# Products of the second group of 32 inverted blocks, moved from stages 3 and 4 of the last head pair to stages 5 and 6

## The chip, the cores and the metric

One NeuronCore of one Trainium2 chip runs the whole kernel. The metric is device time in microseconds (us) for one execution. Engines are named as in the profile: PE (TensorE matmuls), PEld (its weight loads), DVE (VectorE), ACT (ScalarE), POOL (GpSimd), SP (SyncE, which issues most DMAs). Each engine works through its own list of instructions in order, and waits when the next one's input, or the buffer it writes, isn't ready.

## What is computed

One layer of a diffusion transformer on 512 latent tokens and 256 context tokens, model width 1024: normalisation and modulation, one input projection, two groups of heads side by side (neighbourhood attention and a bidirectional RWKV-7 scan), an output projection, and a mixture of 32 experts. The part that matters here is the scan of the second group:

```
def step(S, inp):
    r_t, w_t, kk_t, akk_t, k_t, v_t = inp
    S = (S * w_t[:, :, None, :]
         - jnp.einsum('bhvk,bhk->bhv', S, kk_t)[..., None] * akk_t[:, :, None, :]
         + v_t[..., None] * k_t[:, :, None, :])
    return S, jnp.einsum('bhvk,bhk->bhv', S, r_t)
```

The kernel works it in chunks of 64 tokens. For each chunk, direction and head a 64 x 64 unit triangular matrix has to be inverted; the inverses (tile `TT`, array `TTd` in HBM) are used later, when the scan runs chunk by chunk.

## The kernel before

The program has three long parts: preparation (to about 430 us: normalisation, projections, everything that the scan needs), scan and attention (to about 710 us), and the experts. The change lies in the preparation.

**Pairs, units, stages.** The 8 scan heads are handled as 4 pairs, `p` = 0 to 3 (`rw_pair`). A pair has 4 units: 2 directions by 2 halves of the 12 chunks. The loop over `n` = 2 to 6 in `rw_pair` is what this text calls stages 2 to 6. In stage `n`, `coupling` multiplies out the blocks of unit `n - 3` (PE, tile `pmg`; DVE copies the diagonal blocks masked into `ND`, ACT the others into `NO`), `decayed` makes the operands `AR` and `BK` of unit `n - 2` (ACT, DVE, POOL), and `decay` starts unit `n - 1` (PE tiles `psg` and `paf`, ACT, and a scan on DVE into `sig`).

**The inversion.** Units deliver 96 blocks in all, which are inverted in three groups of 32 (b = 0, 1, 2); group 1 is complete late in pair 2, group 2 in stage 6 of pair 3. `solve_a` inverts the 32 x 32 diagonal blocks of a group by elimination on DVE alone: a transpose into `Mc`, a copy into `Tc`, 30 steps of two instructions each (`tmp` <- `Mc`, `Tc`, then `Tc` <- `Tc`, `tmp`), and two transposes into `Ta` and `Tn`. `solve_b` multiplies `NO` by `Tn` on PE (tile `pp`, 64 small matmuls) and ACT copies the result to `P1`; `solve_c` multiplies `P1` with `Ta` for half a group (32 small matmuls), ACT assembles the half in `TT`, with zeros from POOL, and a DMA writes it to `TTd`.

**The order.** PE's instructions stay in the order in which the code writes them. `fill(us)` takes the next pieces of other work for PE (here attention projections, tile `ipn`, one tile `ip`, and modulation vectors, tile `pm`) worth so many us. The table `SOLVE_B` says in which pair and stage a group's products stand: `solve_b` and the first half in the first place given, the second half in the second. The steps of `solve_a` are written between the pieces of other work; whatever is left of them is written just ahead of `solve_b`. On DVE, ACT, POOL and SP a list scheduler settles the order when the program is built, so code written later can come earlier there. In stage 6 of the last pair the rest of the modulation vectors (`mods`), all of `solve_a` for group 2 and 6 us of other work (`END_FILL`) stand ahead of the table's entry; 16 us of other work (`LAST`) follow, and then the products of group 2.

Helper functions record most instructions, so in the rows nearly all PE matmuls have line L244 and the rest L213: go by the tiles.

Of the kernel before, what the change touches and what calls it, by code (L numbers as in the profile page):

```python
# [8 lines left out]
F32 = mybir.dt.float32  # L9
# [172 lines left out]
FILLS = ((17.23, 9.32, 4.14, 4.14, 4.14, 4.14, 6.22), (14.0, 9.0, 4.1, 4.7, 4.0, 4.0, 6.0), (14.0, 9.0, 4.1, 4.7, 4.0, 4.0, 6.0), (4, 3.13, 3, 2.72, 3.13, 3, 0.0))    # L182
END_FILL = (4, 2)  
RATE = {1: 1.5, 2: 0.8}
SOLVE_B = {(2, 3): (0, 0), (2, 4): (0, 1), (3, 3): (1, 0), (3, 4): (1, 1)}
FIRST = ('k0', 'r0', 'v0')
ITEMS = (('k1', 'r1', 'v1', 'nk0'), ('k2', 'r2', 'v2', 'nq0'), ('k3', 'r3', 'v3', 'nv0'), ('nk1', 'gd', 'nq1', 'nv1'))  
MODGAP = 3.43  
# [39 lines left out]
class K:  # L228
# [426 lines left out]
    def rw_pair(s, p):  # L655
# [34 lines left out]
        for n in range(2, 7):  # L690
# [7 lines left out]
            if n == 6 and p == 3:  # L698
                s.all(s.mods)
                s.all(s.solve_a(p, s.NO))  # L700
                s.fill(sum(END_FILL))
            if (p, n) in SOLVE_B:
                b, half = SOLVE_B[p, n]
                if half == 0:
# [117 lines left out]
    def solve_b(s):  # L822

        PB = s.PB
        s.all(s.solving or ())
        s.solving = False
        NO, Ta, Tn = s.inverse
        lo, hi = s.LO, s.HI
        s.P1 = PB.tile([128, 32, 32], F32, name="P1", tag="Tc")
        for z in range(2):  # L830
            pq = s.ps(tag='pr', name="pp1")
            for k in range(16):
                u = 16 * z + k
                for h in range(2):
                    s.mm(pq[hi[h], 32 * k:32 * k + 32], NO[lo[h], u], Tn[lo[h], u])
            for h in range(2):
                s.act(s.P1[hi[h], 16 * z:16 * z + 16].rearrange("p u c -> p (u c)"), pq[hi[h], :])

    def solve_c(s, b, z):

        nc, PB = s.nc, s.PB
        NO, Ta, Tn = s.inverse
        P1, lo, hi = s.P1, s.LO, s.HI
        TT = PB.tile([128, 16, 64], F32, name="TT", tag="Mc" if b == 2 and z else "TT")

        g0, parts = 32 * b + 16 * z, []
        g = g0
        while g < g0 + 16:
            n = min(12 - g % 12, g0 + 16 - g)
            parts.append((g // 24, g // 12 % 2, g % 12, g - g0, n))  # L850
            g += n
        pq = s.ps(tag='pr', name="pp2")
        for p, d, a, k0, n in parts:
            src = Tn if d else Ta
            ro = hi if d else lo
            for k in range(k0, k0 + n):
                u = 16 * z + k
                for h in range(2):
                    l, r = (Ta, P1) if d else (P1, Ta)
                    s.mm(pq[ro[h], 32 * k:32 * k + 32], l[hi[h], u], r[hi[h], u])  # L860
            us, ks = slice(16 * z + k0, 16 * z + k0 + n), slice(k0, k0 + n)
            for q in range(4):
                rr, o = slice(32 * q, 32 * q + 32), 32 * (q % 2)
                s.act(TT[rr, ks, o:o + 32], src[rr, us])
                if q % 2 != d:
                    nc.gpsimd.memset(TT[rr, ks, 32 - o:64 - o], 0.0)
        for p, d, a, k0, n in parts:
            ro, ks = hi if d else lo, slice(k0, k0 + n)
            for h in range(2):
                s.act(TT[ro[h], ks, (0 if d else 32):(32 if d else 64)],  # L870
                      pq[ro[h], 32 * k0:32 * k0 + 32 * n].rearrange("p (u c) -> p u c", c=32))
        for p, d, a, k0, n in parts:
            for x, y in s.runs(d, a, a + n, d):
                (s.nc.scalar if b == 2 else s.nc.sync).dma_start(s.at(s.TT, d, x, y)[:, :, d, p].rearrange("c p f -> p c f"),
                                                                 TT[:, k0 + x - a:k0 + y - a])
# [1153 lines left out]
```

## Time and profile before

| | us |
|---|---|
| time, median of 3 runs | 1200.48 |
| runs | 1197.87 to 1200.89 |
| the profiled execution, its own time | 1198.07 |
| its span, first to last instruction | 1196.3 |
| PE busy | 1091.7 (91%) |
| DVE busy | 633.8 (53%) |
| ACT busy | 403.2 (34%) |
| POOL busy | 247.0 (21%) |

Times in the rows are counted from the start of the span. The shares are averages over parts with different limits: what a change in the preparation is worth is read from the waits there.

### The profile page before, as it was taken

What the parts mean: (1) busy time and instruction counts of PE and PEld (TensorE: products, weight loads), DVE (VectorE), ACT (ScalarE), POOL (GpSimd) and SP (SyncE); (2) the same over time, 40 slices, a digit from 0 to 9 for tenths busy, and PEclk for the clock granted to TensorE, in tenths of its full rate; (3) what the DMA queues carried; (4) which work ended last, traced back from release to release, by engine and by line L of the source; (5) the groups of instructions that cost most, each with busy time, mean ns of one, the idle gap of its engine ahead of it and who ended that gap; (6) DMA issues with size and microseconds to landing.
All of it is one profiled execution on the core that took longest, in us unless ns stands there. A gap on an engine that the chain in (4) does not pass through costs nothing.

```text
span 1196.3 us, 23890 instructions
## 1 busy us (share of the span) xinstructions
PE 1091.7 (91%) x9673; PEld 762.6 (64%) x9674; DVE 633.8 (53%) x1384; ACT 403.2 (34%) x780; POOL 247.0 (21%) x283
## 2 busy tenths in 40 slices
PE   3899999969587689999998979999999999999996
PEld 1677777748466678888776754646464646464644
DVE  5745567986938523554578782333333333333335
ACT  3543546347373534555322251111111111120200
POOL 0664465524334100020253030000000000000000
PEclk9999999979878787999999989999999999999998
DMA  9544655446434278764353939999999999999995
GB/s 370 174 132 142 192 188 178 144 129 186 136 87 166 68 213 225 220 179 107 103 144 119 364 123 365 409 409 409 408 409 409 408 409 408 409 409 409 407 409 188
DMA packets 148797, 310.00 MB, mean 259 GB/s; under 512 B 32323, under 2 KB 71107, under 8 KB 148684
## 3 DMA queue, kind: packets, MB, share of 16 engines
q1 hardware_dynamic: 142860, 305.82, 71.4%
q10 hardware_dynamic: 5792, 2.62, 0.8%
q8 instruction: 77, 1.26, 0.4%
q14 instruction: 36, 0.29, 0.1%
q0 software_dynamic: 32, 0.00, 0.0%
HBM read 283.22 MB, written 25.17 MB: 258 GB/s over the span
## 4 chain that ended last, share of the span: by engine, by line
PE 65%; DVE 19%; DMA 7%; ACT 4%; issue 2%; POOL 2%; SPq 0%; ACTq 0%; DVEq 0%; POOLq 0%
PE ph L244 16%; PE py L244 8%; PE psc L244 7%; PE ip L244 7%; PE pga L244 4%; DMA wt<-in_w_dram 4%; PE ipn L244 4%; DVE Tc L213 4%; DVE tmp L213 3%; PE pgr L244 3%; PE pr L244 2%; PE pm L244 1%; PE ppt L248 1%; PE pon L244 1%; ACT TT L213 1%
## 5 line engine op out<-in xcount | busy, mean ns | idle before, releaser
L244 PE MATMUL ph<-wt,HS 128*64 128x512 f32 x1024 | 224.6, 593 | 0.4 <-DMA wt<-in_w_dram 0.2
L244 PEld LDWEIGHTS ph<-wt,HS 128*64 128x64 f32 x1024 | 73.5, 137 | 140.7 <-issue 126.4
L213 DVE TENSOR_TENSOR hid<-hid,ph 128x512 f32<-128x512 f32 x16 | 11.0, 688 | 249.6 <-PE ph L244 249.6
L244 PE MATMUL py<-wt,hid 128*64 128x256 f32 x1024 | 114.5, 381 | 0.0
L244 PEld LDWEIGHTS py<-wt,hid 128*64 128x64 f32 x1024 | 71.9, 137 | 40.3 <-issue 3.9
L213 POOL CAST two<-sel 128x128 fp32r<-128x128 f32 x32 | 8.6, 296 | 425.4 <-PE pbc L244 425.4
L213 POOL TENSOR_TENSOR wlo<-wraw,whi 128x512 fp32r<-128x512 f32 x54 | 72.4, 1343 | 111.4 <-ACT whi L213 107.7
L244 PE MATMUL ipn<-whi,hth 128*128 128x256 f32 x256 | 82.2, 321 | 13.6 <-DVE vs L213 9.9
L213 DVE TENSOR_TENSOR x<-psc,x 128x512 f32<-128x512 f32 (+1 forms) x136 | 78.6, 650 | 0.0
L244 PE MATMUL ipn<-wlo,hth 128*128 128x256 f32 x256 | 77.4, 302 | 0.0
L244 PE MATMUL ipn<-whi,htl 128*128 128x256 f32 x256 | 76.8, 300 | 0.0
L244 PE MATMUL ip<-hth,whi 128*128 128x512 f32 (+1 forms) x200 | 74.7, 374 | 1.4 <-ACT nr L213 1.3
L244 PE MATMUL ip<-htl,whi 128*128 128x512 f32 (+1 forms) x200 | 71.3, 357 | 0.7 <-DVE htl L213 0.7
L244 PE MATMUL ip<-hth,wlo 128*128 128x512 f32 (+1 forms) x200 | 71.3, 356 | 0.0
L244 PEld LDWEIGHTS ipn<-whi,hth 128*128 128x128 f32 x256 | 54.1, 211 | 22.2 <-issue 19.4
L244 PE MATMUL pga<-OH,xh 128*128 128x256 f32 x240 | 60.1, 291 | 0.9 <-DVE OH L213 0.9
L244 PE MATMUL pga<-OH,xl 128*128 128x256 f32 x240 | 59.2, 287 | 0.0
L244 PE MATMUL psc<-yh,oht 128*128 128x512 f32 (+1 forms) x136 | 54.5, 405 | 1.2 <-DVE x L213 0.8
L213 ACT ACTIVATE hid<-pth 128x512 f32<-128x512 f32 x16 | 9.6, 599 | 133.3 <-PE pth L248 133.3
L244 PEld LDWEIGHTS ipn<-wlo,hth 128*128 128x128 f32 x256 | 54.2, 212 | 0.0
L244 PEld LDWEIGHTS ipn<-whi,htl 128*128 128x128 f32 x256 | 54.2, 212 | 0.0
L244 PE MATMUL psc<-yl,oht 128*128 128x512 f32 (+1 forms) x136 | 51.4, 381 | 0.1
(351 smaller groups left out, 2235.9 us busy)
## 6 DMA issues: line engine op xcount, KB each, us to landing
wt<-in_w_dram SPq DMA_DIRECT2D x384, 512.0 KB
wm<-in_wmod_dram SPq DMA_DIRECT2D x48, 512.0 KB
wraw<-in_w_in_dram SPq DMA_DIRECT2D x30, 256.0 KB
wraw<-in_w_na_dram SPq DMA_DIRECT2D x24, 256.0 KB
BKj<-BKd SPq DMA_DIRECT2D x12, 512.0 KB
BKd<-BK SPq DMA_DIRECT2D x12, 384.0 KB
ARz<-ARd SPq DMA_DIRECT2D x16, 256.0 KB
wo<-in_w_out_dram SPq DMA_DIRECT2D x16, 256.0 KB
```

The lines of the kernel that those rows point to most:

```text
L213: i = f(*a, **k)
L244: i = s.nc.tensor.matmul(out, l, r, start=start, stop=stop)
L248: i = s.nc.tensor.transpose(out, x, s.ident if ident is None else ident)
```

## The change

The two entries of group 1 in `SOLVE_B` move: its products stand in stages 5 and 6 of pair 3, no longer in stages 3 and 4. Since `solve_a` of group 2 now comes between the two halves of group 1 in the code, `solve_c` takes `Ta`, `Tn` and `P1` from a note that `solve_b` leaves (`s.halved`), not from the latest inversion.

```diff
-SOLVE_B = {(2, 3): (0, 0), (2, 4): (0, 1), (3, 3): (1, 0), (3, 4): (1, 1)}
+SOLVE_B = {(2, 3): (0, 0), (2, 4): (0, 1), (3, 5): (1, 0), (3, 6): (1, 1)}
...
-        s.P1 = PB.tile([128, 32, 32], F32, name="P1", tag="Tc")
+        P1 = PB.tile([128, 32, 32], F32, name="P1", tag="Tc")
+        s.halved = Ta, Tn, P1
...
-                s.act(s.P1[hi[h], 16 * z:16 * z + 16].rearrange("p u c -> p (u c)"), pq[hi[h], :])
+                s.act(P1[hi[h], 16 * z:16 * z + 16].rearrange("p u c -> p (u c)"), pq[hi[h], :])
...
-        NO, Ta, Tn = s.inverse
-        P1, lo, hi = s.P1, s.LO, s.HI
+        Ta, Tn, P1 = s.halved
+        lo, hi = s.LO, s.HI
```

No instruction is added or taken away by it; their places change. Three of these, in the order of the built programs (- before, + after):

PE, stage 3 of pair 3, right behind the decay of unit 2 (`psg`, `paf`):

```order
 L244 MATMUL paf<-ad_613,uph 128x384
 L244 MATMUL paf<-ad_613,upl 128x384
-L244 MATMUL pp_3713<-Tn,NO 32x32 x32
-L244 MATMUL pp_3748<-Tn,NO 32x32 x32
-L244 MATMUL pp_3784<-Ta,P_3712 32x32 x8
-L244 MATMUL pp_3784<-P_3712,Ta 32x32 x24
 L244 MATMUL ipn<-whi,hth_110 128x256
 L244 MATMUL ipn<-wlo,hth_110 128x256
```

The 96 matmuls of `solve_b` and the first half are gone from here; other work follows the decay directly.

PE, stage 5 of pair 3, right behind the coupling of unit 2 (`pmg`):

```order
 L244 MATMUL pgt<-mr,ctb 1x512
 L244 MATMUL pmg<-BK,AR 32x64 x24
+L244 MATMUL pp_3879<-Tn,NO 32x32 x32
+L244 MATMUL pp_3914<-Tn,NO 32x32 x32
+L244 MATMUL pp_3950<-Ta,P_3878 32x32 x8
+L244 MATMUL pp_3950<-P_3878,Ta 32x32 x24
 L244 MATMUL ipn<-whi,hth_113 128x256
 L244 MATMUL ipn<-wlo,hth_113 128x256
```

The same 96 matmuls stand here now, with the couplings of units 1 and 2 and the decay of unit 3 ahead of them. The 32 of the second half move from stage 4 to the end of stage 6 in the same way.

DVE, the last steps of the elimination of group 1 in pair 3 (`b_3860`, `AR`, `BK` and `af` are the operands of unit 3):

```order
+L213 SCALAR_TENSOR_TENSOR b_3860<-af,kk 128x384
 L213 TENSOR_TENSOR tmp<-Mc,Tc 128x58
+L213 SCALAR_TENSOR_TENSOR AR<-kk,Ep 128x6x64
 L213 TENSOR_TENSOR Tc<-Tc,tmp 128x2x29
+L213 SCALAR_TENSOR_TENSOR BK<-b_3860,Em 128x6x64
+L213 TENSOR_TENSOR af<-af,ks 128x384
 L213 TENSOR_TENSOR tmp<-Mc,Tc 128x30
 L213 TENSOR_TENSOR Tc<-Tc,tmp 128x30
 L213 STREAM_TRANSPOSE Ta<-Tc 128x32x32
+L213 TENSOR_TENSOR ND<-pmg,ctb 128x192
 L213 STREAM_TRANSPOSE Tn<-Tc 128x32x32
```

Work of units 1 to 3 that stood behind the transposes now stands between the elimination's steps: seven instructions in all ahead of `Tn` (the five of unit 3 with its scan into `sig`, and `ND` of units 1 and 2).

## Rows read from the trace of the kernel before

**Rows 1.** Busy time by stretch, PE, PEld, DVE, ACT, POOL, then granted clock, DMA

```profile
318.00:332.50 14.50, 0.59 (x2) 0.18 (x1) 13.98 (x29) 4.59 (x12) 2.71 (x4) 0.64 0.37 114
332.50:344.00 11.50, 11.46 (x270) 10.17 (x270) 0.00 (x0) 7.09 (x14) 0.02 (x1) 0.56 0.29 71
...
367.00:387.00 20.00, 17.48 (x107) 16.06 (x107) 19.04 (x35) 8.35 (x14) 10.44 (x8) 0.84 0.44 149
387.00:404.00 17.00, 11.14 (x103) 10.55 (x104) 16.32 (x45) 4.96 (x12) 3.22 (x3) 0.90 0.11 42
404.00:416.00 12.00, 9.90 (x263) 9.43 (x258) 3.31 (x4) 10.02 (x24) 1.62 (x2) 0.57 0.43 115
```

**Rows 2.** Waits from 318 to 420 us: total us, times, longest

```profile
PE pp L244 <- DVE Tn L213: 13.9, 1, 13.9
...
DVE ND L213 <- PE pmg L244: 11.7, 1, 11.7
...
PE pp L244 <- DVE nst L213: 5.7, 1, 5.7
...
PEld pnt L248 <- ACT nx L213: 3.6, 1, 3.6
```

**Rows 3.** The chain that ended last, 318 to 445 us: start, us, what

```profile
330.68 1.73 DVE Tn L213
332.54 4.97 PE pp L244 x190
337.50 2.86 PE ipn L244 x12
...
354.33 2.36 PE ip L244 x9
356.69 0.81 PE pmg L244 x48
...
358.58 4.68 DMA wm<-in_wmod_dram
...
401.62 1.85 DVE Tn L213
```

**Rows 4.** DVE in order of time, 319 to 326 us: start, us, operation

```profile
319.64 0.34 DVE L213 TENSOR_TENSOR ND<-pmg,ctb 128x192 f32<-128x192 f32 x1
...
321.31 0.96 DVE L213 TENSOR_TENSOR_SCAN sig<-cut,sig 128x390 f32<-128x390 bf16 x1
...
322.42 0.56 DVE L213 SCALAR_TENSOR_TENSOR b<-af,kk 128x384 f32<-128x384 f32 x1
...
323.11 0.55 DVE L213 SCALAR_TENSOR_TENSOR AR<-kk,Ep 128x384 f32<-128x384 f32 x1
...
324.53 0.54 DVE L213 SCALAR_TENSOR_TENSOR BK<-b,Em 128x384 f32<-128x384 f32 x1
...
325.20 0.54 DVE L213 TENSOR_TENSOR af<-af,ks 128x384 f32<-128x384 f32 x1
```

**Rows 5.** The start of group 2's elimination on DVE

```profile
362.73 1.93 DVE L213 STREAM_TRANSPOSE Mc<-ND 128x1024 f32<-128x1024 f32 x1 [1.55 <-PE pm L244]
```

**Rows 6.** DVE beside POOL: two like operations, one while POOL works

```profile
381.11 0.40 DVE L213 TENSOR_TENSOR tmp<-Mc,Tc 128x234 f32<-128x234 f32 x1
...
381.39 1.30 POOL L213 TENSOR_TENSOR wlo<-wraw,whi 128x512 fp32r<-128x512 f32 x1 [1.50 <-ACT whi L213]
...
381.54 1.41 DVE L213 TENSOR_TENSOR Tc<-Tc,tmp 128x234 f32<-128x234 f32 x1
```

**Rows 7.** POOL, 352 to 356 us

```profile
352.62 0.41 POOL L213 TENSOR_TENSOR AR<-rs,Ep 128x128 f32<-128x128 f32 x1
353.00 1.26 POOL L213 TENSOR_TENSOR row<-row,mr 1x512 f32<-1x512 f32 x1
355.22 0.92 POOL L213 TENSOR_TENSOR BK<-af,Em 128x384 f32<-128x384 f32 x1 [0.96 <-DVE af L213]
```

**Rows 8.** The experts' weight loads: count, ns min/median/max, first and last start us

```profile
L213 SPq DMA_DIRECT2D wt<-in_w_dram x384: 327/328/1181, 652.0 to 1168.0; - x192
```

## The prediction

> **What bounds the kernel now.** Start with the busy times by stretch and look only at the end of the preparation. From 318 to 332.5 us PE is busy for 0.59 of 14.5 us while DVE is busy for 13.98; in the next stretch, to 344, it is the other way round: PE 11.46 of 11.5, DVE nothing at all [rows 1]. Two engines that take turns like this are tied by a wait in each direction. The view of waits names them: PE's products (`pp`) waited 13.9 us in one piece for `Tn`, the last transpose of group 1's elimination on DVE, and after that DVE's `ND` waited 11.7 us for `pmg`, the next coupling, which stands behind those products in PE's order [rows 2]. The chain of work that ended last runs straight through: DVE until `Tn` is done at 332.4, PE's products 4.97 us, twelve `ipn`, later nine `ip`, the last coupling at 356.69, a load of `wm` of 4.68 us, and then group 2's elimination until `Tn` of group 2 is done at 403.5 [rows 3]. There PE waits once more, 5.7 us, behind the last DVE operations [rows 2].
>
> So the bound from 318 to 404 is DVE's elimination, twice, with a piece between them in which DVE has little to do. The second elimination lasts from 362.73 [rows 5] to 403.47 [rows 3], 40.7 us, and can't start before the coupling of the last unit. What counts for the time is when that coupling (356.69) is done; whatever PE does meanwhile is worth nothing by itself.
>
> **What the change does to this, step by step.**
>
> *PE's wait of 13.9 us in stage 3.* The products no longer stand there, so PE goes on at 318.6 with 27 `ipn`, one `pm`, the coupling of unit 1, the decay of unit 3, 24 `ipn`, a gate row and the coupling of unit 2. In the trace these fill PE from 337.50 [rows 3] to about 351, at the lower clock for the first half, with the second half's products among them: 11 to 13 us, so PE comes to the moved products at 330 to 331.
>
> *`Tn` of group 1 gets later.* DVE is already full up to 332.4 (13.98 of 14.5), and now seven more instructions stand ahead of `Tn`: two `ND` at 0.34, the scan 0.96, `b` 0.56, `AR` 0.55, `BK` 0.54, `af` 0.54 [rows 4]: 3.8 us. POOL's part of unit 3 and one weight split come under the elimination too, and there DVE loses time: of two operations of the same size, the one without POOL beside it took 0.40 us, the one beside a 1.30 us `wlo` 1.41 [rows 6], 1.0 us or 0.78 of POOL's duration. For `wlo` 1.30, `AR` 0.41 and `BK` 0.92 [rows 6, 7] that makes 2.0 us; POOL's `row`, 1.26, I put beside the two transposes at no cost, as `Mc` took 1.93 us while POOL worked beside it [rows 5], no more than the 1.85 of a `Tn` [rows 3]. The Trainium skill (SBUF — State Buffer, Who interferes with whom) has a stricter rule: a DVE instruction with two SBUF inputs and a POOL instruction that reads SBUF never share, and the second to start waits for the whole of the first; with one input DVE goes free. By that rule the three would cost up to 2.6 us and the gain in the sum below would be 6.8; the rows agree with it in kind, and in size up to when each operation began. By the rows, `Tn` is then done at 332.4 + 3.8 + 2.0 = 338.2. Bounds: 336.2 without any of POOL's effect, 341 if PE or ACT hold up unit 3's scan by some 3 us, since six steps of the elimination are queued behind it on DVE.
>
> *PE still waits, but for 7 to 8 us, and elsewhere.* From 331 to 338.2. Both waits of similar and greater length in the trace leave the clock low: the stretches behind them ran at a mean granted clock of 0.56 and 0.57 [rows 1], mostly the lower of the two levels, 1.2 GHz. I take the same here.
>
> *From `Tn` to the last coupling.* Before, 24.3 us (332.4 to 356.69). In the new order only the products (4.97), twelve `ipn` (2.86) and nine `ip` lie between. The first two durations are at the lower clock already; the nine `ip` took 2.36 at the full one [rows 3], up to twice that at the lower, and I take 3.3. Sum 11.1, so the last coupling starts at 349.3 instead of 356.69: 7.4 us earlier. Bounds: at the full clock half of 4.97 and of 2.86, and 2.36, together 6.3; all at the lower clock 12.6.
>
> *From there to the second elimination.* 6.0 us before (356.69 to 362.73), ended by `pm` [rows 5] behind its load [rows 3]. The two loads still go out when the first `pm` has read its buffers, which stands behind the coupling in both orders; they shift with it. DVE's small operations on `nst` shift too, as the copies ahead of them follow the same `ipn`.
>
> *The second elimination* keeps its steps, 40.7 us. Under it PE now has the 32 matmuls of the second half: 32 of 190 such in 4.97 us is 0.8 us, and PE's spare 5.7 us at the end covers them. Of their twelve ACT copies eight are queued ahead of the copy into `Tc`, but ACT waits there for `pm` anyway; ACT is busy for 8.35 of 20 us in this stretch [rows 1]. Without cover PE would be late by 0.8.
>
> *The last products.* In the built order five `TT` copies that ACT did after the copies of `P1` for group 2 now stand ahead of them; 1.8 us by their sizes if PE had to wait for it. ACT is busy for 10.02 of 12 us there [rows 1] and PE then waits for its `nx` [rows 2]: the sum of ACT's work sets the end, and it is the same. I take 0, with 1.8 as the bound.
>
> *All later work* shifts with PE. The experts run on weight loads whose first goes out at 652.0 [rows 8], long after the scan's first steps, and is released by the program's progress; nothing in between is tied to a fixed moment.
>
> **Sum.** 7.4 us earlier. The profiled execution took 1198.07 (1.8 us of it outside the span): 1190.7. Its own time is 2.4 below the median of the runs, so a median could come out anywhere from there to 1193; I say 1191. Bounds of the gain: late `Tn` 341, all PE at the lower clock, and the 1.8 on ACT leave 356.69 - 341 - 12.6 - 1.8 = 1.3; early `Tn` 336.2 and the full clock give 356.69 - 336.2 - 6.3 = 14.2.
>
> **Rivals.**
>
> *POOL costs more.* If every POOL operation beside the elimination costs its whole duration, `row` beside the transposes too, it is 1.30 + 0.41 + 1.26 + 0.92 = 3.9 instead of 2.0: gain 5.5, time 1192.6. For it: the 1.0 us of the row is what one overlap cost that began when part of the POOL operation was done. Against it: the `Mc` row.
>
> *The clock holds.* If 7 us of waiting don't lower it, 6.3 instead of 11.1 after `Tn`: gain 12, time about 1186. Against it stand the two stretches at 0.56 and 0.57.
>
> *The wait only moves.* The 13.9 us turn up again at stage 5 and the last coupling hardly moves. That needs `Tn` at 342 or later, 3.8 us beyond my sum: unit 3's scan would have to wait for PE or ACT, whose order now decides about DVE. For it: DVE is full and gets work. Against it: PE reaches unit 3's decay some 6 us after 318.6, and the elimination's steps ahead of the scan run to about 328. Gain 0 to 3.5, time 1196 to 1198.
>
> *Slower.* The second half's results now go out through SP's queue behind the writes of `nx` and ahead of weight loads, from which ACT and POOL make `whi` and `wlo` for PE; and POOL's zeros for the next `TT` wait for that write. If this holds PE up by more than its spare 5.7 us, PE ends the filler after `Tn` of group 2. From 5.7 - 0.8 + 7.4 = 12.3 us on it is slower than before; one weight load waits at most some 5 us, as `wm` did (4.68). It would have to happen three times; at four, 1203.
>
> **Chances.** My sum with its nearer bounds (1187 to 1195): 0.61. POOL costs more: 0.10. The clock holds: 0.11. The wait only moves: 0.12. Slower: 0.06. What a measurement of this kernel can tell from no change is about 0.3%, 3.6 us. Faster by more: 0.61 + 0.10 + 0.11 = 0.82; within: 0.12; slower: 0.06. The range takes in the first three cases and part of the fourth: 1185.5 to 1196.5, all on one side of 1200.48.
>
> **What would show it.** In the profile after: no wait of PE near 318; PE waiting some 7 us for `Tn` behind the coupling of unit 2, `Tn` done near 338; the last coupling near 349 and `Mc` near 355; the second elimination 40 to 41 us long, PE still waiting 4 to 5 us at its end. I am wrong if `Tn` is done after 342, if `Mc` waits for something other than `pm`, or if PE no longer waits at the end of the second elimination, so that something else sets it.

## The result, and the profile after

| | before | changed |
|---|---|---|
| time, median (executions) | 1200.68 (4) | 1185.83 (4) |
| executions | 1197.87 to 1203.79 | 1182.67 to 1190.86 |
| ratio, 95% interval | | 0.988, 0.9837 to 0.9922 |
| the profiled execution | 1198.07 | 1190.86 |

The change makes the kernel faster, as forecast, by 0.8 to 1.6%. The profiled pair differs by 7.2 us, nearly the 7.4 of the sum; the medians differ by twice that. Where the rest lies is the question of the experiments.

Busy time by stretch after the change (PE, PEld, DVE, ACT, POOL, then granted clock, DMA share, GB/s):

```profile
268.50:276.00 7.50, 7.50 (x46) 6.54 (x47) 2.06 (x3) 5.85 (x14) 2.62 (x3) 0.65 0.32 73
318.00:332.50 14.50, 13.05 (x209) 9.40 (x208) 14.19 (x28) 6.51 (x15) 5.90 (x8) 1.00 0.62 185
332.50:344.00 11.50, 5.15 (x193) 5.09 (x194) 6.77 (x12) 7.89 (x18) 3.06 (x4) 0.62 0.20 59
```

Against [rows 1]: from 318 to 332.5 PE works beside DVE, 13.05 us instead of 0.59, at the full clock. The stretch in which it is short of work is now the next one. The first line is for later: it belongs to the head of the program.

The waits from 310 to 415 us (total, times, longest):

```profile
PE pp L244 <- DVE Tn L213: 7.8, 1, 7.8
...
PE pp L244 <- DVE nst L213: 2.9, 1, 2.9
...
DVE ND L213 <- PE pmg L244: 1.3, 1, 1.3
...
POOL wlo L213 <- DMA TTd<-TT: 12.4, 1, 12.4
```

Against [rows 2], 13.9 us have become 7.8 (forecast 7 to 8), DVE's 11.7 for the coupling 1.3, PE's 5.7 at the end of the second elimination 2.9 (forecast 4 to 5). POOL's 12.4 is new; it ends at 349.21, and `Mc` of group 2 waits for `pm` on PE and not for what follows on POOL.

The places of the prediction, in order of time on DVE and PE: 

```profile
285.53 2.12 DVE L213 STREAM_TRANSPOSE Mc<-ND 128x1024 f32<-128x1024 f32 x1
...
336.90 1.89 DVE L213 STREAM_TRANSPOSE Tn<-Tc 128x1024 f32<-128x1024 f32 x1
...
349.77 0.88 PE L244 MATMUL pmg<-BK,AR 64*32 64x64 f32 x48
...
355.61 1.94 DVE L213 STREAM_TRANSPOSE Mc<-ND 128x1024 f32<-128x1024 f32 x1 [1.75 <-PE pm L244]
...
394.07 1.86 DVE L213 STREAM_TRANSPOSE Tn<-Tc 128x1024 f32<-128x1024 f32 x1
...
416.82 1.06 PE L244 MATMUL pgr<-ARz,BKj 128*64 128x128 f32 x8 [0.81 <-DMA ARz<-ARd]
...
421.53 0.69 DVE L213 COPY Rs<-pr 128x512 f32<-128x512 f32 x1 [1.05 <-PE pr L244]
```

`Tn` of group 1 is done at 338.79 (forecast 338.2), the last coupling starts at 349.77 (349.3), the second elimination at 355.61 (about 355) and lasts 40.3 us. The copy into `Rs` is DVE's first step of the scan; it serves as a mark below.

### The profile page after: what moved, and what is told of

Read it like the earlier page. It is cut to its first block, busy times and chain, and to the rows that moved or that the text cites. A ratio compares the mean times of both kernels' runs of the same rounds, so it can differ in the third digit from the quotient of the medians.

```text
span 1189.1 us, 23896 instructions
## 1 busy us (share of the span) xinstructions
PE 1094.2 (92%) x9673; PEld 764.3 (64%) x9674; DVE 632.4 (53%) x1384; ACT 402.8 (34%) x780; POOL 246.2 (21%) x283
## 4 chain that ended last, share of the span: by engine, by line
PE 51%; DVE 7%; DMA 6%; ACT 1%; issue 1%; SPq 0%; POOL 0%; ACTq 0%; DVEq 0%; POOLq 0%
PE ph L244 17%; PE py L244 9%; PE psc L244 6%; PE pga L244 5%; DMA wt<-in_w_dram 3%; PE pgr L244 2%; PE pr L244 2%; PE acc L244 1%; PE pon L244 1%; PE ppt L248 1%; DMA V<-NVd 1%; DVE fst L213 1%; PE po L244 1%; DVE x L213 1%; DVE oacc L213 1%; PE pkb L248 1%
## 5 line engine op out<-in xcount | busy, mean ns | idle before, releaser
L244 PEld LDWEIGHTS py<-wt,hid 128*64 128x64 f32 x1024 | 71.9, 137 | 40.3 <-issue 3.9
```

The source lines that it names most:

```text
L244: i = s.nc.tensor.matmul(out, l, r, start=start, stop=stop)
```

## The experiments

**Theory.** Time follows the last coupling: it starts the second elimination, and everything later shifts with that. **Rivals.** PE's removed wait is the gain, wherever the products go; or later loads, which differ between executions, decide what is left of it.

Executions differ by several us, the head of the program among other places. So beside the time each kernel is read by one stretch of its trace, from the start of `Mc` of group 1 to the first `Rs` (421.53 - 285.53 = 136.0 above), which holds all that the change moves:

| kernel | that stretch, us | time, median (executions) | ratio, 95% interval |
|---|---|---|---|
| before, first and second trace | 146.0, 145.2 | 1199.0 to 1200.9 | |
| changed, three traces | 136.0, 136.0, 134.8 | 1185.83 (4), 1188.61 (6), 1188.78 (1) | 0.990, 0.9868 to 0.9932 (the six) |
| fourth and fifth stage | 144.5 | 1199.99 (12) | 0.9989, 0.9965 to 1.0013 |
| both halves in the fifth | 142.3 | 1192.56 (9) | 0.9936, 0.9913 to 0.9959 |
| behind the last coupling | 139.8 | 1193.29 (12) | 0.9932, 0.9905 to 0.9958 |
| writes on ACT's queue | 139.6 | 1193.26 (7) | 0.9932, 0.9905 to 0.9959 |
| 18 matmuls in the wait | 137.2 | 1190.12 (11) | 0.9931, 0.9905 to 0.9958 |
| 36 matmuls in the wait | 135.8 | 1189.58 (6) | 0.9917, 0.989 to 0.9944 |
| modulation earlier | 134.3 | 1186.59 (6) | 0.9881, 0.9858 to 0.9904 |
| filler earlier | 131.7 | 1186.04 (6) | 0.9876, 0.9843 to 0.9908 |
| filler and modulation earlier | 130.4 | 1182.25 (6) | 0.9854, 0.982 to 0.9887 |

The times were taken on several chips, each kernel's ratio against the kernel before on the same chip. Stretch and time go together, all but for a few us among the middle ones: some 15 us between the ends of the one column, 18 of the other. From the first `Rs` to the end of the span, the fourteen traces take 761.0 to 768.6 us, with no tie to the change (before 765.9 and 767.1, changed 767.6, 764.2 and 763.7).

**The changed kernel again**, unaltered.

> The changed kernel unaltered, to learn how much of its gain repeats. The theory of the prediction (the second elimination starts when the last coupling is done, and all later work shifts with it): Mc near 355.6 us and the end 7 us earlier than before, so the profiled execution at 1190 and a ratio near 0.994. First rival (the later loads NVd, V and KTd of the scan differ from execution to execution and hide part of the gain): Mc again near 355.6, but the load of V shorter than the 14.61 us of the first trace, and the end 9 to 14 us earlier, 1184 to 1189, ratio 0.988. Second rival (the gain in the elimination itself varies): Mc well ahead of 355.6, by some 5 us.

Measured: `Mc` at 355.69, span 1185.9, ratio 0.990 with an interval that leaves out 0.994: the first rival. The load of V in the chain of the first trace, and in that of this one (start, us, what):

```profile
435.02 14.61 DMA V<-NVd
```

```profile
431.08 6.79 DMA V<-NVd
```

The first trace gave back some 4 us there: its third copy into `Rs` stands 45.6 us behind the first (467.14), 41.0 in this one (462.68).

**A third trace of it.**

> The changed kernel, unaltered, for a third trace. Theory: Mc of group 2 at 355.3 to 356, its Tn near 394, in the scan the first COPY into Rs at 421.5 to 421.8 and the load of V near 7 us as in the second trace (the 14.61 of the first being one execution's), the end 1185 to 1187 in the span. Rival: the long load of V is a feature of the new order and comes back in every second execution; then 12 to 15 us again and the span near 1189.

Neither quite: `Mc` at 357.27 since its head ran late (`Mc` of group 1 at 288.35), the load of V 11.6 us, span 1186.9. So that load is long in some executions and not in others; it is part of the spread, not of the order.

**The kernel before again**, unaltered.

> The kernel before, unaltered, for a second trace of it. In its first trace the granted clock came back to full at 270.9 us (matmuls of 0.41 us become 0.28) and the coupling of the third stage stood at 316.23; in five traces of kernels with the same order up to there it came back at 272 to 275 and the coupling stood at 317.2 to 318.4. Theory: that is a difference between executions, the first trace of before was an early one, and the gain of the change against a usual execution is larger by it than the sum. Then this trace has Mc of group 1 near 285.5 instead of 284.37, the third-stage coupling at 317.5 to 318.5, Mc of group 2 at 364 to 365 instead of 362.73, and the time 1199 to 1201. Rival: the change itself delays the clock; then all of it repeats the first trace within 0.4 us up to 362.73.

Measured: as the theory said in the head and the time (1199.7), `Mc` of group 2 at 363.42, a little early. The stretch from 268.5 to 276 in the first trace of before and in the second:

```profile
268.50:276.00 7.50, 7.50 (x96) 6.73 (x96) 2.71 (x3) 6.18 (x15) 2.95 (x3) 0.84 0.32 73
```

```profile
268.50:276.00 7.50, 7.50 (x47) 6.60 (x46) 2.14 (x3) 5.79 (x14) 2.61 (x3) 0.66 0.32 73
```

PE is busy throughout in both; the granted clock is 0.84 in one and 0.66 in the other, as in the changed kernel (0.65). The trace from which the sum was made had an early head, by 1.1 us at `Mc` of group 1 (284.37 and 285.46). The changed kernel's later head is no effect of the change: the kernel before has it too.

**Half of the move.**

```diff
-SOLVE_B = {(2, 3): (0, 0), (2, 4): (0, 1), (3, 5): (1, 0), (3, 6): (1, 1)}
+SOLVE_B = {(2, 3): (0, 0), (2, 4): (0, 1), (3, 4): (1, 0), (3, 5): (1, 1)}
```

> Half of the move: the products at the fourth and fifth stage instead of the fifth and sixth. The theory: Tn of group 1 is done near 338 as with the whole move, but 24 ipn, a gate row, one more coupling and the second half's products now stand between it and the last coupling, so this comes some 18 to 20 us after Tn instead of 11, at 356 to 358, Mc at 362 to 364, and the time is that of the kernel before within 3 us (1197 to 1203). Rival, what is gained is PE's wait at the third stage: that wait falls here too, from 13.9 to some 11 us, and the time is 3 us or more below before. Rival, part of the gain comes from the second half's results leaving later: nothing of it here, since they leave only one stage later.

Its chain of work, with DVE's `Mc` behind it:

```profile
336.65 1.73 DVE Tn L213
338.51 4.97 PE pp L244 x190
343.49 5.43 PE ipn L244 x24
```

```profile
363.35 1.96 DVE L213 STREAM_TRANSPOSE Mc<-ND 128x1024 f32<-128x1024 f32 x1 [0.34 <-PE pm L244]
```

`Tn` is done at 338.38, as late as after the whole move, the 24 `ipn` stand behind the products, and `Mc` comes at 363.35: no gain, and the interval holds 1. PE's wait has left stage 3, is 12.2 us long instead of 13.9, and nothing came of it. From `Tn` to the last coupling it takes 17.0 us here, 11.0 after the whole move: what counts is what stands between the two.

**The second half not moved on.** 

```diff
-SOLVE_B = {(2, 3): (0, 0), (2, 4): (0, 1), (3, 5): (1, 0), (3, 6): (1, 1)}
+SOLVE_B = {(2, 3): (0, 0), (2, 4): (0, 1), (3, 5): (1, 2)}
...
-                if half == 0:
+                if half in (0, 2):
...
-                s.solve_c(b, half)
+                for x in ((0, 1) if half == 2 else (half,)):
+                    s.solve_c(b, x)
```

> Both halves of the products at the fifth stage; the second half isn't moved on under the second elimination. Theory: its 32 matmuls now lie between Tn and the last coupling, 0.8 us at full clock and up to 1.3 at the lower, so the coupling comes at 350.5 to 351.2 instead of 349.8, Mc 0.7 to 1.4 later, and in return PE's wait at the end of the second elimination grows from 2.9 us by as much; time 0 to 1.5 us above the changed kernel's. Rival: the second half under the elimination, with its twelve ACT copies, is what holds ACT at the end; then the last products end earlier against Tn of group 2 and the time falls by 1 us or more.

Slower than either expected: 142.3 us in the stretch, 6 to 7.5 more than the changed kernel. From `Tn` (336.79) to the coupling it is 13.0 us instead of 11.0, to `Mc` 7.1 instead of 5.8, the elimination 42.2 instead of 40.3, from its `Tn` to the first `pgr` 22.8 instead of 20.9:

```profile
349.77 0.87 PE L244 MATMUL pmg<-BK,AR 64*32 64x64 f32 x48
...
355.82 0.98 PE L244 MATMUL pm<-wm,scc 128*32 128x256 f32 x8 [4.18 <-DMA wm<-in_wmod_dram]
```

```profile
356.85 1.90 DVE L213 STREAM_TRANSPOSE Mc<-ND 128x1024 f32<-128x1024 f32 x1 [3.95 <-PE pm L244]
```

So the second half's later place is worth far more than its matmuls: four steps each grow by 1.2 to 2 us without it, and only some 3 of the 10 us in the stretch are left as gain. Which of its copies, writes and zeros does that wasn't tried apart. The chain of before has a hint: between the products and the last coupling it runs through twelve copies into `TT` on ACT, one behind the other from 346.56 to 351.40, which the prediction's reading of the chain passes over.

**The filler of stage 5 ahead of the wait.**

```diff
-FILLS = (..., (4, 3.13, 3, 2.72, 3.13, 3, 0.0))
+FILLS = (..., (4, 3.13, 3, 2.72, 6.13, 0, 0.0))
```

> The 3 us of filler of the fifth stage (nine ip, the row after them) is done in the fourth, before PE's wait for Tn and not after it. The theory: PE waits some 3 us less for Tn, Tn stays near 338.8 or comes up to 1 us later, only the products lie between it and the last coupling, which comes at 344 to 345 instead of 349.8, Mc at 350 to 351, and the time is 5 us below that of the changed kernel. Rival, the load of wm sets Mc and not the coupling: Mc moves by less than 2 us. Rival, the later loads give the end: Mc early, the scan at the same moments as in the changed kernel.

```profile
338.09 2.21 PE L244 MATMUL pp<-Tn,NO 32*32 32x32 f32 x128 [0.43 <-DVE Tn L213]
...
342.95 1.50 PE L244 MATMUL pmg<-BK,AR 64*32 64x64 f32 x48
...
349.79 1.08 PE L244 MATMUL pm<-wm,scc 128*32 128x256 f32 x8 [3.47 <-DMA wm<-in_wmod_dram]
```

```profile
350.93 1.93 DVE L213 STREAM_TRANSPOSE Mc<-ND 128x1024 f32<-128x1024 f32 x1 [6.05 <-PE pm L244]
```

PE hardly waits for `Tn`, and only the products stand between it and the coupling: 342.95, earlier than expected, and `Mc` at 350.93 as the theory said, since it then waits for `pm` and this for the load of `wm`. The stretch is 4 us shorter, and the first `Rs` stands at 417.00 instead of 421.53, so neither rival holds. The time, 1186.04, isn't told apart from the changed kernel's.

**Two modulation steps earlier.** 

```diff
+            if n == 5 and p == 3:
+                next(s.mods, None)
+                next(s.mods, None)
             if (p, n) in SOLVE_B:
```

> The changed kernel with two of the last four modulation steps (eight pm) ahead of the moved products, so that the last two loads of wm go out before the last coupling; the filler stays where it was. Theory: PE does them in its wait for Tn, the last coupling stays at 349.5 to 350, Mc comes 1 to 2 us behind it at 351.5 to 352.5 instead of 355.6, and Tn of group 2 as much earlier, 391 to 392; PE's wait at the end (2.9 us) is then used up, so the scan starts 2 to 4 us earlier and the time is 1184 to 1186. Rival: something else holds Mc (the chain of nst on DVE, or the copy into Tc): Mc at 354 or later and no gain.

`Mc` comes 0.6 us behind its `ND` and no longer waits for `pm`. It stands at 353.42 in a trace whose head was 2.9 us late: from `Tn` (340.92) to `Mc` 12.5 us instead of 16.8. Under the elimination PE now meets another wait, for DVE:

```profile
PE ipn L244 <- DVE rot L213: 7.0, 1, 7.0
```

It was 2.5 us in the changed kernel. The elimination took 43.1 us instead of 40.4, and 1.3 us of the stretch remained as gain; the time, 1186.59, isn't told apart from the changed kernel's.

**Both together.** The last two edits, in one kernel.

> As the run with the fifth stage's filler ahead of the wait, and two of the last four modulation steps (eight pm, and with them the last two loads of wm) also ahead of the products. In that run Mc stood at 350.93, 6.05 us behind its ND, for pm behind a load of wm. Theory: the loads are then there in time, the last pm ends some 2 us after the last coupling, Mc comes at 346 to 347, 4 to 5 us earlier. What is gained in the end is limited by PE, whose spare wait at the end of the second elimination was 4.3 us: the wait falls to 0 to 1 us, the scan starts 3 to 4.5 us earlier, the time is 1181 to 1184. Rival: as behind the last coupling alone, ACT's or PE's queue takes the gain back, PE waits for a copy of nr instead, and the scan starts no earlier than in that run, 1186 or more.

```profile
348.32 1.91 DVE L213 STREAM_TRANSPOSE Mc<-ND 128x1024 f32<-128x1024 f32 x1 [0.65 <-PE pm L244]
```

`Mc` at 348.32 doesn't wait for the load any more, but comes 1.3 to 2.3 us later than expected. PE loses them within the products, by ACT's `P1` and by a pause for which the profile shows no cause:

```profile
341.85 0.24 PE L244 MATMUL pp<-Ta,P 32*32 32x32 f32 x2 [0.91 <-ACT P L213]
...
344.96 0.85 PE L244 MATMUL pp<-P,Ta 32*32 32x32 f32 x22 [1.73 <-issue]
```

The first `Rs` comes at 415.57, 1.4 us ahead of the run with the filler alone, where 3 to 4.5 were expected. The time is 1182.25, ratio 0.9854: the fastest kernel here, clearly better than before and in its median better than the changed one, though the two intervals overlap. It lies in the range expected; against the run with the filler alone the stretch is 1.3 us shorter and the median 3.8, and where the rest comes from isn't shown.

**All products behind the last coupling.** (`steps_of(a, 32)` does the first 32 steps of `a`; its definition is left out here.)

```diff
-SOLVE_B = {(2, 3): (0, 0), (2, 4): (0, 1), (3, 5): (1, 0), (3, 6): (1, 1)}
+SOLVE_B = {(2, 3): (0, 0), (2, 4): (0, 1)}
...
-                s.all(s.solve_a(p, s.NO))
-                s.fill(sum(END_FILL))
+                s.all(s.solving or ())
+                s.solving = False
+                a = s.solve_a(p, s.NO)
+                s.steps_of(a, 32)
+                s.solve_b()
+                s.solve_c(1, 0)
+                s.solve_c(1, 1)
+                s.all(a)
+                s.fill(sum(END_FILL))
```

> Both halves of group 1's products go behind the last coupling, the last modulation matmuls and the issue of group 2's elimination, so nothing that needs Tn of group 1 stands between PE and the last coupling. The theory (only the last coupling counts): the coupling at about 336 instead of 349.8, Mc at about 342 instead of 355.6, the second elimination again 40 to 41 us, its Tn done at about 383 and the time 12 us below that of the changed kernel, about 1174 to 1177. Rival, PE is by then the bound: Mc is early all the same, but PE has lost the cover of its spare 2.9 us and ends the filler after Tn of group 2; gain 4 to 8 us, 1178 to 1182. Rival, the later loads give the end: Mc and Tn early as above, but the scan's first steps start at the same moments as in the changed kernel, gain 0 to 3 us.

The coupling stood at 337.27, near the theory's 336, but `Mc` came at 347.26 and not at 342: the `pm` ahead of it waited 7.0 us for the load of `wm`. `Tn` of group 2 was done at 389.40, 6.5 us ahead of the changed kernel; the first `Rs` stood 3.8 us behind the changed kernel's. ACT and then PE in order of time:

```profile
387.72 1.27 ACT L213 ACTIVATE TT<-Ta 32x256 f32<-32x256 f32 x3 [5.95 <-DVE Ta L213]
...
390.72 0.60 ACT L213 ACTIVATE nr<-ipn 128x512 f32<-128x512 f32 x1
```

```profile
391.37 0.58 PE L244 MATMUL ipn<-whi,hth 128*128 128x256 f32 x1 [7.40 <-ACT nr L213]
```

In ACT's order the copies of `Ta` into `TT`, which wait for the end of the elimination, stand ahead of a copy of `nr` that PE needs to go on. PE stands still for 7.4 us, and has 66 more `ipn` to do after `Tn` than in the changed kernel, where they were done beside the elimination; the first `pgr` comes 31.2 us behind `Tn` instead of 20.9. The coupling isn't all that counts, then: the theory holds while PE's other work ends before the elimination does.

**The writes of `TTd` on ACT's queue.**

```diff
-(s.nc.scalar if b == 2 else s.nc.sync)
+(s.nc.scalar if b >= 1 else s.nc.sync)
```

> The results of group 1's products (TTd) are written through ACT's queue instead of SP's, so that no weight load stands behind them; it costs ACT five issues of some 0.38 us each. The prediction's slower rival (writes on SP's queue hold the weight loads and through them PE): the time falls, by 2 us or more, and PE's wait at the end of the second elimination grows. The theory: nothing waited for these writes that counts; the time is that of the changed kernel, 1186 to 1189, at most 2 us more for ACT.

Slower by 4 us in the stretch and some 5 in the median, with intervals that overlap. `Mc` (354.79) was no later, the elimination took 43.1 us, and PE waited 6.8 us for `rot` under it. PE's wait at the end of the elimination shrank to 1.4 us where the rival had it grow: SP's queue, the prediction's way to a slower kernel, was no burden that this relieved. The orders of DVE and ACT shifted with the edit, so it doesn't price the five issues alone.

**Matmuls in the wait.** 18, then 36 (`range(12)` in place of `range(6)`), whose results nobody reads:

```diff
+                if half == 0 and b == 1:
+                    for _ in range(3):
+                        pk = s.ps((128, 384), tag='pr', name="pbusy")
+                        for _ in range(6):
+                            s.mm(pk, s.uph[:, 0, 0], s.low[0][0][:, 0:384])
                 if half == 0:
                     s.solve_b()
```

> The changed kernel with 18 matmuls more, whose results nobody reads, ahead of the moved products, where PE waits 7.8 us for Tn; the order of everything else is as it was. They ask what the low granted clock after the wait costs. The prediction's bounds: with the wait 11.1 us from Tn to the last coupling, at the full clock 6.3. Theory: the clock stays full, the wait shrinks to 1 to 3 us, Tn stays at 338.5 to 339, the last coupling comes at 345 to 346 instead of 349.8, Mc at 351 to 352 behind the load of wm, and the time is 3 to 4 us below the changed kernel's. Rival: ACT's copies between the two halves of the products set this stretch and not the clock; then the matmuls are shorter, the coupling comes at 348 or later, and the time is the same within 2 us.

They took 3.4 us, not 6; the wait for `Tn` was still 4.6 us, and from `Tn` to the coupling it took 10.6. So they didn't answer the question.

> As the run with 18 idle-filling matmuls, with 36 of them: there the 18 took 3.41 us, not the 6 that was reckoned, PE still waited 4.6 us for Tn, and the granted clock behind that wait was low as before (0.65 in 332.5 to 344). 36 should take 6.8 us and leave a wait of about 1 us. Theory: with a wait this short the clock stays full, the products and the twelve ipn run at their short durations, the last coupling follows Tn in 6.5 to 8 us instead of 11.0, Mc comes 3 to 4 us earlier against Tn than in the changed kernel. Rival: the clock falls all the same, or ACT's copies set the stretch: 10 us or more from Tn to the coupling. The time is a weak witness, since executions of the run with 18 spread from 1184.5 to 1200.

```profile
329.52 6.55 PE L244 MATMUL pbusy<-th,uph 128*128 128x384 f32 x36
337.72 2.31 PE L244 MATMUL pp<-Tn,NO 32*32 32x32 f32 x128 [1.65 <-DVE Tn L213]
340.39 0.31 PE L244 MATMUL pp<-Ta,P 32*32 32x32 f32 x2 [0.36 <-ACT P L213]
341.01 0.47 PE L244 MATMUL pp<-Ta,P 32*32 32x32 f32 x9 [0.30 <-ACT P L213]
...
343.05 0.41 PE L244 MATMUL ipn<-wlo,hth 128*128 128x256 f32 x1
...
348.08 0.87 PE L244 MATMUL pmg<-BK,AR 64*32 64x64 f32 x48
```

With 1.65 us of waiting left, the first 128 `pp` take 2.31 us where the changed kernel needs 3.46 for 122 of them. Then PE waits for ACT's copies into `P1`, so that from the first `pp` to the first `ipn` (342.67) it is 4.95 us, against 4.90 in the changed kernel. The `ipn` behind run at 0.41 us each, as in the changed kernel; the same shape takes 0.28 at the full clock. 10.5 us from `Tn` (337.58) to the coupling instead of 11.0, the stretch 135.8: the rival. The granted clock by stretches (0.50 is the lower of the two levels), in the changed kernel's wait, in this run, and in the run with the filler earlier:

```profile
331.00:335.00 4.00, 0.05 (x4) 0.00 (x0) 3.93 (x12) 2.95 (x6) 1.25 (x3) 1.00 0.37 112
336.00:338.80 2.80, 0.00 (x0) 0.00 (x0) 2.80 (x4) 1.56 (x5) 0.81 (x1) 0.50 0.44 141
```

```profile
336.10:339.60 3.50, 1.88 (x119) 1.91 (x121) 2.02 (x2) 3.02 (x8) 0.00 (x0) 1.00 0.13 38
340.00:346.00 6.00, 5.34 (x79) 5.01 (x79) 0.00 (x0) 4.57 (x10) 0.00 (x0) 0.50 0.26 57
```

```profile
337.60:340.60 3.00, 2.27 (x134) 2.10 (x128) 2.82 (x10) 2.22 (x5) 0.00 (x0) 1.00 0.28 94
341.00:344.00 3.00, 2.71 (x102) 2.65 (x106) 0.76 (x5) 2.92 (x7) 2.02 (x3) 0.50 0.00 0
```

In the changed kernel the clock fell within the wait. With the wait filled it fell all the same, between 339.6 and 340.0, while PE worked on the products; the waits of 0.36 and 0.30 us came behind that. With the filler earlier it fell behind waits of 0.43 and 0.37 us. The Trainium skill (TensorE: Matmul & The Clock Gate, A second HAM failure mode: psum-queue depth-cycling) tells of another kernel in which short idle times between groups of matmuls made the clock swing between its two levels. The run with the filler earlier agrees with it; in the run with 36 matmuls the wait of 1.65 us stood ahead of the fall, and what caused it isn't shown.

## Why the prediction came out as it did

The mechanism was right in the main: the products left the place where PE and DVE waited for each other, the last coupling came earlier by about the forecast, and the second elimination with it. The sum was too small by 2.6 us, and the execution that it was taken from had an early head. The terms, from the two traces of before and the three of the changed kernel (means):

| step | before | changed | difference | predicted |
|---|---|---|---|---|
| `Mc` of group 1 to the end of its `Tn` | 48.2 | 53.0 | +4.8 | +5.8 |
| `Tn` to the last coupling | 23.7 | 10.9 | -12.8 | -13.2 |
| last coupling to `Mc` of group 2 | 6.2 | 5.7 | -0.5 | 0 |
| the second elimination | 40.7 | 40.4 | -0.3 | 0 |
| its `Tn` to the first `pgr` | 22.0 | 20.8 | -1.2 | 0 |
| first `pgr` to first `Rs` | 4.7 | 4.7 | 0 | 0 |
| sum | 145.6 | 135.6 | -10.0 | -7.4 |

*PE's wait.* Gone, and 7.8 us of it back at stage 5, as said. That it is worth nothing by itself is borne out by half of the move, where it left stage 3 too and the time stayed, and by the 36 matmuls, where it shrank to 1.65 us and the stretch stayed.

*`Tn` later by 5.8.* Measured 4.8. The seven durations were added in full, but DVE's instructions overlap at their ends: the `ND` before `Tn` starts at 336.64, takes 0.33, and `Tn` starts at 336.90. POOL's effect is there:

```profile
326.79 1.49 POOL L213 TENSOR_TENSOR wlo<-wraw,whi 128x512 fp32r<-128x512 f32 x1 [0.66 <-ACT whi L213]
...
327.03 1.65 DVE L213 TENSOR_TENSOR af<-af,ks 128x384 f32<-128x384 f32 x1
```

`af` took 1.65 us instead of the 0.54 of [rows 4]. 1.1 us for a `wlo` of 1.49 is 0.75 of its duration, near the 0.78 from [rows 6]. The stricter rule that the prediction quoted, in which `af` waits for the end of `wlo`, would end it at 326.79 + 1.49 + 0.54 = 328.82; it ended at 328.68. Rule and row are 0.14 us apart here. The rival in which POOL costs more needed 3.9 us for POOL and a loss beside the transposes. Both are out: the seven durations less some 0.08 us of overlap each are 3.2, which leaves about 1.6 of the 4.8 for POOL; and `Ta`, with POOL's `BK` and `row` beside it, took 1.93 us, where `Tn`, with POOL idle, took 1.89:

```profile
334.86 1.93 DVE L213 STREAM_TRANSPOSE Ta<-Tc 128x1024 f32<-128x1024 f32 x1
```

```profile
334.63 0.96 POOL L213 TENSOR_TENSOR BK<-af,Em 128x384 f32<-128x384 f32 x1 [1.14 <-DVE tmp L213]
335.55 1.26 POOL L213 TENSOR_TENSOR row<-row,mr 1x512 f32<-1x512 f32 x1
```

*`Tn` to the last coupling.* The value was right, 11.0 in the first trace for 11.1, and the clock did fall in PE's wait. That the wait is why the stretch takes so long was not borne out: with the wait filled it is nearly as long, 10.5. The prediction let the products' 4.97 us halve at the full clock; but they take 4.9 us with their first 128 at either level, since ACT's copies stand between. So its bound of 6.3 is too low. By an estimate from rows the full clock would leave some 8.8: 4.9 for the products, 1.5 for twelve `ipn` that start 0.12 us apart, as they do at the full clock in these traces, and 2.36 for the nine `ip`. The rival in which the clock holds is refuted by the changed kernel's own trace (0.50 from 336, `ipn` at 0.41, 11.0 us and not 6.3). Its time, about 1186, is nevertheless the median that was measured: the time alone would have pointed to the wrong case.

*The second elimination.* The prediction priced the second half's matmuls at 0.8 us, as 32 of 190. The 190 are records, two for each of the 96 matmuls; the second half has 64 of them, and they took 1.75 us under the elimination (371.52 to 373.27). That fits PE's wait at its end, which was 5.7 and 4.4 us in the two traces of before and fell to 2.9, below the 4 to 5 expected. The wait covered the matmuls, so the sum didn't suffer.

*The last products, 0.* Here the sum was furthest off against its bounds: I looked for a loss of up to 1.8 and there was a gain of 1.2. ACT at the end of the second elimination, after the change:

```profile
395.96 1.69 ACT L213 ACTIVATE TT<-Tn 32x256 f32<-32x256 f32 x4
397.67 1.26 ACT L213 ACTIVATE TT<-Ta 32x128 f32<-32x128 f32 x4
...
399.49 2.43 ACT L213 ACTIVATE P<-pp 32x512 f32<-32x512 f32 x4
...
407.62 1.21 ACT L213 ACTIVATE nx<-pnt 128x256 fp32r<-128x256 f32 x4 [0.44 <-PE pnt L248]
```

The four small copies of `Ta` are done while ACT would wait for the products; `nx` comes 11.7 us behind `Tn` (395.93), in the first trace of before 12.35 (415.82 behind 403.47). That is 0.7 us. More comes from PE's clock behind it. PE waits 1.49 us for `nx` instead of 3.19, and of the 54 `ipn` that follow up to `pgr` one is longer than 0.28 us, where 18 were before (9 in the second trace of before). First before, then after:

```profile
417.50:421.00 3.50, 3.50 (x20) 3.50 (x19) 0.00 (x0) 1.21 (x4) 2.72 (x4) 0.53 0.76 226
```

```profile
409.30:416.00 6.70, 6.70 (x57) 6.50 (x55) 0.00 (x0) 1.21 (x4) 2.70 (x4) 1.00 0.88 252
```

From the first of these `ipn` it is 6.7 us to the end of the last; before, it is 8.1 to the `pgr` that follows at once. After the change PE then waits 0.81 us for the load of `ARz`, so that 0.7 + 1.4 - 0.8 gives the 1.3 us between the two first traces. That the sum of ACT's work sets the end is thus the step that failed: PE's clock has a part in it, and the sum had no term for that.

*The second half's place.* The sum leaves the steps behind the last coupling as they were, wherever the second half stands. With both halves in the fifth stage they grow by 1.2, 1.9 and 1.9 us, so a good part of the gain hangs on this. Why stays open.

*The wait only moves; slower.* Neither came. POOL's 12.4 us behind the write of `TTd` is the wait that the slower rival named, but `Mc`, `Tn` of group 2 and PE's end of filler all came early.

*The point.* 1191 was forecast, the median was 1185.83, inside the range by 0.3 us, which is luck. So is the agreement of the profiled pair with the sum, 7.2 and 7.4 us: there the stretch gained 10.0, the head was 1.2 later, and the part behind the first `Rs` took 1.7 longer. 2.6 us of the difference are the terms above. The rest is spread between executions: the changed kernel's eleven executions here run from 1182.67 to 1193.59 with a median of 1188.1, and the execution of before that the sum started from, 1198.07, lies below that kernel's usual 1199 to 1201. The medians differ by some 12 us, the stretch by 10.0; the interval of the six executions, 0.9868 to 0.9932 or 8 to 16 us, holds both. Which part of the scan makes the rest I can't say, since the untraced executions show only their time.

## What to carry to other kernels

Where two engines wait for each other in turn, ask what stands between the end of one's work and the start of its next, and shorten that; the wait itself may only change its place. Moving the independent filler ahead of the wait, and the loads that the next step needs, adds to it. Before a sum of a few us is set against one trace, see how late that trace's head was: a second trace of the same kernel told that in one run. And the gain ends when another engine's order takes over: with the products behind the last coupling this coupling was earliest, and ACT's order made it a loss of some 4 us of the stretch against the changed kernel.

## Not expected of the hardware

PE's granted clock came back to full at different moments in two traces of one program, with PE busy throughout (0.84 and 0.66 of the stretch from 268.5 to 276), and `Mc` of group 1 stands 1.1 us later in the second. 36 matmuls that kept PE busy up to 1.65 us before the products didn't keep the twelve `ipn` behind them at their 0.28 us: they ran at 0.41, and the granted clock fell while PE was at work. The same load of V took 14.6, 6.8 and 11.6 us in three executions of one kernel.
